# Row softmax in 17 groups: the scaling multiply moved from VectorE to GpSimd, except in the last three groups

## The chip, the cores and the metric

The kernel runs on one core of a Trainium2 chip. The metric is the device time of one execution in microseconds (us). Each figure is the median of three runs. For the kernel before it is 161.42 us, with the three runs between 161.40 and 161.58 us. The profile is of one further execution, which took 161.41 us; the profiled span inside it is 159.6 us, so some 1.8 us of the measured time lie outside the span. All times in profile lines count from the start of that span.

## What is computed

The reference is a softmax over the last axis of a float32 array of 16 x 1024 x 512, that is, over 16384 rows of 512 numbers:

```python
def reference(x):                       # x: (16, 1024, 512) float32
    x_max = np.max(x, axis=-1, keepdims=True)
    exp_x = np.exp(x - x_max)
    return (exp_x / np.sum(exp_x, axis=-1, keepdims=True)).astype(np.float32)
```

The array is 33.55 MB. It is read once and the result, of the same size, is written once.

## The kernel before

The 16384 rows are spread over 128 partitions, so each partition handles 128 rows of 512 numbers. In what follows "a row" means one such row on all 128 partitions at once: a tile of 128 x 512 numbers, 256 KB. The rows come in ten chunks. The second number of each pair is the place in the SBUF buffer, which holds 96 rows; the last two chunks reuse places of earlier ones.

```python
CHUNKS = [
    (3, 0), (5, 3), (8, 8), (16, 16), (16, 32), (16, 48), (16, 64), (16, 80), (16, 0), (16, 16),
]
EARLY = 8                          # chunks 0 to 7 are loaded at once
AFTER_STORE = {2: [8], 3: [9]}     # chunk 8 is loaded after the store of chunk 2, chunk 9 after that of chunk 3
GROUP = 8
FINISH_BEFORE = (1, 2, 3)
STORE_ROWS = {3: 8, 4: 8, 5: 8}
```

Work goes by groups of at most eight rows: one group of 3, one of 5, and fifteen of 8, numbered 0 to 16. Chunks of 16 rows are two groups. In chunks 3, 4 and 5 each group is stored by itself; in chunks 6 to 9 the store waits for both groups.

Each group passes through three steps. VectorE takes the negated maximum of each row. ScalarE computes the exponentials in place, one instruction per row, and with it the row sums. VectorE then takes the reciprocals of the sums and multiplies each row by its own. The load instructions are issued from SyncE's queue, the store instructions from ScalarE's:

```python
    def rowmax(g):
        ...
        nc.vector.reduce_max(out=shift[g], in_=place[k][:, a:b, :], axis=AX, negate=True)

    def exps(g):
        ...
        for r in range(a, b):
            nc.scalar.activation(
                out=place[k][:, r, :], in_=place[k][:, r, :], func=EXP,
                bias=shift[g][:, r - a : r - a + 1], scale=1.0,
                accum_out=sums[g][:, r - a : r - a + 1],
            )

    def scale(g):
        ...
        nc.vector.reciprocal(out=recip, in_=sums[g])
        for r in range(a, b):
            nc.vector.tensor_scalar_mul(
                out=place[k][:, r, :], in0=place[k][:, r, :],
                scalar1=recip[:, r - a : r - a + 1],
            )
        if since is not None:
            nc.scalar.dma_start(out=dst[k][:, since:b, :], in_=place[k][:, since:b, :])
        ...
```

Each engine works through its instructions in the order of the program. The order is that of this loop: scale of a group comes one group late, after the exponentials of the next; only ahead of chunks 1, 2 and 3 is the group in hand finished first.

```python
        for g, (k, a, _, _) in enumerate(groups):
            if waiting is not None and a == 0 and k in FINISH_BEFORE:
                scale(waiting)
                waiting = None
            rowmax(g)
            exps(g)
            if waiting is not None:
                scale(waiting)
            waiting = g
        scale(waiting)
```

A store instruction stands in ScalarE's order and waits there until the rows are scaled, so the exponentials behind it wait too.

Of the kernel before, what the change touches and what calls it, by code (L numbers as in the profile page):

```python
# [1 line left out]

# [4 lines left out]

F32 = mybir.dt.float32
EXP = mybir.ActivationFunctionType.Exp
AX = mybir.AxisListType.X  # L10


CHUNKS = [
    (3, 0), (5, 3), (8, 8), (16, 16), (16, 32), (16, 48), (16, 64), (16, 80), (16, 0), (16, 16),
]
SBUF_ROWS = 96

EARLY = 8
AFTER_STORE = {2: [8], 3: [9]}

GROUP = 8

FINISH_BEFORE = (1, 2, 3)

STORE_ROWS = {3: 8, 4: 8, 5: 8}

ON_ACT = ()

AT_HEAD = {mybir.EngineType.SP: 3}

def loads_at_the_head(nc):

    main, body = nc.main_func.blocks[0], nc.main_func.blocks[1]
    for engine, count in AT_HEAD.items():
        loads = [
            i
            for i in body.instructions
            if i.engine == engine and type(i).__name__ == "InstDMACopy"  # L40
        ][:count]
        barrier = next(
            n
            for n, i in enumerate(main.instructions)
            if i.engine == engine and type(i).__name__ == "InstDrain"
        )
        for load in loads:
            body.instructions.remove(load)
        main.instructions[barrier:barrier] = loads


def one_barrier_on_exit(nc):


    end = nc.main_func.blocks[2].instructions

    def of(engine, kind):
        return [i for i in end if i.engine == engine and type(i).__name__ == kind]

    for engine in (  # L60
        mybir.EngineType.Activation,
        mybir.EngineType.PE,
        mybir.EngineType.DVE,
        mybir.EngineType.SP,
    ):
        arrivals = [i for i in of(engine, "InstDrain") if i.has_update()]
        leaves = of(engine, "InstEventSemaphore")
        assert len(arrivals) == len(leaves) == 2
        end.remove(leaves[0])
        end.remove(arrivals[1])  # L70
    gather, release, gather_2, release_2 = of(mybir.EngineType.Pool, "InstEventSemaphore")
    end.remove(release)
    end.remove(gather_2)

@with_exitstack
def kernel(
    ctx: ExitStack,
    tc: tile.TileContext,
    x: bass.AP,
    out: bass.AP,  # L80
):
    nc = tc.nc
    nc.at_finalize(loads_at_the_head)
    nc.at_finalize(one_barrier_on_exit)
    P = nc.NUM_PARTITIONS

    x_flat = x.flatten_outer_dims()
    out_flat = out.flatten_outer_dims()
    n, d = x_flat.shape
    assert n == P * sum(R for R, _ in CHUNKS)  # L90


    src, dst, at = [], [], 0
    for R, _ in CHUNKS:
        for flat, views in ((x_flat, src), (out_flat, dst)):
            part = flat[at : at + P * R, :]
            views.append(part.rearrange("(p r) d -> p r d", r=R))
        at += P * R

    data = ctx.enter_context(tc.tile_pool(name="data", bufs=1))  # L100
    stats = ctx.enter_context(tc.tile_pool(name="stats", bufs=4))
    held = data.tile([P, SBUF_ROWS, d], F32, name="held")
    place = [held[:, s : s + R, :] for R, s in CHUNKS]


    groups = []
    for k, (R, _) in enumerate(CHUNKS):
        m = -(-R // GROUP)
        cuts = [R * i // m for i in range(m + 1)]
        since = 0  # L110
        for a, b in zip(cuts, cuts[1:]):
            ends = b == R or b - since >= STORE_ROWS.get(k, R)
            groups.append((k, a, b, since if ends else None))
            since = b if ends else since
    shift = [None] * len(groups)
    sums = [None] * len(groups)

    def load(k):
        queue = nc.scalar if k in ON_ACT else nc.sync
        queue.dma_start(out=place[k], in_=src[k])  # L120

    def rowmax(g):
        k, a, b, _ = groups[g]
        shift[g] = stats.tile([P, b - a], F32, name="shift", tag="shift")
        nc.vector.reduce_max(  # L125
            out=shift[g], in_=place[k][:, a:b, :], axis=AX, negate=True
        )

    def exps(g):
        k, a, b, _ = groups[g]  # L130
        sums[g] = stats.tile([P, b - a], F32, name="sums", tag="sums")
        for r in range(a, b):
            nc.scalar.activation(  # L133
                out=place[k][:, r, :],
                in_=place[k][:, r, :],
                func=EXP,
                bias=shift[g][:, r - a : r - a + 1],
                scale=1.0,
                accum_out=sums[g][:, r - a : r - a + 1],
            )  # L140

    def scale(g):
        k, a, b, since = groups[g]
        recip = stats.tile([P, b - a], F32, name="recip", tag="recip")
        nc.vector.reciprocal(out=recip, in_=sums[g])  # L145
        for r in range(a, b):
            nc.vector.tensor_scalar_mul(  # L147
                out=place[k][:, r, :],
                in0=place[k][:, r, :],
                scalar1=recip[:, r - a : r - a + 1],  # L150
            )
        if since is not None:
            nc.scalar.dma_start(
                out=dst[k][:, since:b, :], in_=place[k][:, since:b, :]
            )
        if b == CHUNKS[k][0]:
            for later in AFTER_STORE.get(k, ()):
                load(later)

    with tc.manual_schedule():  # L160
        for k in range(EARLY):
            load(k)
# [13 lines that stand above are left out]
# [1 line left out]
_INS = ['x']  # L177
_OUTS = [((16, 1024, 512), 'float32')]


# [23 lines left out]
```

## Time and profile before

| what | value |
|---|---|
| device time, median of 3 | 161.42 us (161.40 to 161.58) |
| profiled span | 159.6 us |
| VectorE busy | 123.9 us (78% of the span) |
| ScalarE busy | 93.3 us (58%) |
| GpSimd busy | 0.2 us (four small memsets) |
| bytes moved by DMA | 67.13 MB, 421 GB/s over the span |
| last store issued at | 144.93 us |

Busy times are sums of instruction durations per engine. The DMA line of the profile gives, for 40 equal slices of the span, how busy the 16 DMA engines were on average, in tenths; the line below it gives the rate of bytes moved. A groups line names the source line, the engine, the operation, the tiles written and read, the number of instructions, and after the bar the total busy time and the mean duration of one. The chain of work that ended last is followed back from the last instruction, at each step to what released it.

### The profile page before, as it was taken

The page shows a single profiled execution, that of the slowest core. Times are in us where ns is not written, and L with a number is a line of the kernel's source. Part 1 is how long each engine was busy: PE and PEld are TensorE (multiplying, and loading weights), DVE is VectorE, ACT ScalarE, POOL GpSimd, SP SyncE. Part 2 cuts the span into 40 slices and gives each one's busy share as a digit, 9 for nine tenths or more (in the row PEclk, how much of TensorE's full clock was granted, in tenths as well). Part 3 has the DMA queues.
Part 4 walks back from the last instruction along what each step waited for, and adds up shares of the span by engine and source line. Part 5 has one row for each costly group of instructions (what it writes and reads, how often), then busy time and mean ns, then how long its engine had stood idle before and what let it go on. Part 6 is the DMA issues. An engine that isn't in the chain of part 4 may idle for free.

```text
span 159.6 us, 511 instructions
## 1 busy us (share of the span) xinstructions
DVE 123.9 (78%) x162; ACT 93.3 (58%) x257; POOL 0.2 (0%) x4
## 2 busy tenths in 40 slices
DVE  0482880799699999999999999999999999853000
ACT  0717119207994959595958687776868595940000
POOL 0000000000000000000000000000000000000000
DMA  7999999899999999999899999999999999999993
GB/s 267 443 456 432 399 414 466 375 404 467 411 446 411 485 419 396 439 411 493 378 448 439 411 497 411 405 444 402 435 444 485 411 402 468 435 402 419 485 411 164
DMA packets 3315, 67.13 MB, mean 421 GB/s; under 512 B 368, under 2 KB 368, under 8 KB 624
## 3 DMA queue, kind: packets, MB, share of 16 engines
q1 hardware_dynamic: 1440, 33.56, 49.4%
q10 hardware_dynamic: 1872, 33.56, 49.0%
q14 instruction: 3, 0.02, 0.0%
HBM read 33.55 MB, written 33.55 MB: 421 GB/s over the span
## 4 chain that ended last, share of the span: by engine, by line
DVE 71%; ACT 14%; issue 3%; DMA 3%; DVEq 0%; ACTq 0%
DVE shift L125 39%; DVE held L147 30%; ACT held L133 14%; DMA held<-in_x_dram 3%; DVE recip L145 2%; DVEq L199 0%; ACTq L133 0%
## 5 line engine op out<-in xcount | busy, mean ns | idle before, releaser
L133 ACT ACTIVATE held<-held,shift 128x512 f32<-128x512 f32 x128 | 90.5, 708 | 43.4 <-DVE shift L125 33.3
L125 DVE TENSOR_REDUCE shift<-held 128x8 f32<-128x4096 f32 (+2 forms) x17 | 70.7, 4164 | 4.6 <-DMA held<-in_x_dram 4.6
L147 DVE TENSOR_SCALAR held<-held,recip 128x512 f32<-128x512 f32 x128 | 52.2, 482 | 0.6
L133 ACT ACTIVATION_READ_ACCUMULATOR held<-held,shift 128x1 f32 x128 | 23.9, 187 | 0.0
L145 DVE RECIPROCAL recip<-sums 128x8 f32<-128x8 f32 (+2 forms) x17 | 3.3, 195 | 15.8 <-ACT held L133 15.8
L133 ACT ACT_TABLE_LOAD x1 | 1.3, 1283 | 4.7 <-DMA held<-in_x_dram 4.7
L188 POOL MEMSET const-bfloat16-1.0<- 128x1 bf16 x1 | 0.1, 103 | 0.0
L188 POOL MEMSET const-uint8-127<- 128x1 uint8 x1 | 0.1, 102 | 0.0
L188 POOL MEMSET const-float32-1.0<- 128x1 f32 x1 | 0.1, 100 | 0.0
L188 POOL MEMSET const-float32-0.0<- 128x1 f32 x1 | 0.1, 99 | 0.2 <-issue 0.2
## 6 DMA issues: line engine op xcount, KB each, us to landing
held<-in_x_dram SPq DMA_DIRECT2D x7, 4096.0 KB, 41.8
out_dram<-held ACTq DMA_DIRECT2D x4, 4096.0 KB, 20.9
out_dram<-held ACTq DMA_DIRECT2D x7, 2048.0 KB, 35.3
held<-in_x_dram SPq DMA_DIRECT2D x1, 2048.0 KB, 11.7
held<-in_x_dram SPq DMA_DIRECT2D x1, 1280.0 KB, 7.2
out_dram<-held ACTq DMA_DIRECT2D x1, 1280.0 KB, 19.9
held<-in_x_dram SPq DMA_DIRECT2D x1, 768.0 KB, 4.6
out_dram<-held ACTq DMA_DIRECT2D x1, 768.0 KB, 15.6
```

The costliest lines, as they stand in the source:

```text
L125: nc.vector.reduce_max(out=shift[g], in_=place[k][:, a:b, :], axis=AX, negate=True)
L133: nc.scalar.activation(out=place[k][:, r, :], in_=place[k][:, r, :], func=EXP, bias=shift[g][:, r - a : r - a + 1], scale=1.0, accum_out=s ...
L145: nc.vector.reciprocal(out=recip, in_=sums[g])
L147: nc.vector.tensor_scalar_mul(out=place[k][:, r, :], in0=place[k][:, r, :], scalar1=recip[:, r - a : r - a + 1],)
L188: nc = _bacc.Bacc("TRN2", target_bir_lowering=False, num_devices=1)
```

## The change

GpSimd, which has nothing to do in the kernel before, takes over the multiplication of the rows by their reciprocal sums in groups 0 to 13, 104 of the 128 rows. In the last three groups (24 rows) VectorE keeps it. The reciprocals stay on VectorE in all groups. The purpose is to take work from VectorE, the busiest compute engine, and give it to an idle one.

```diff
+ON_VECTOR = 3
 ...
         nc.vector.reciprocal(out=recip, in_=sums[g])
+        engine = nc.gpsimd if g < len(groups) - ON_VECTOR else nc.vector
         for r in range(a, b):
-            nc.vector.tensor_scalar_mul(
+            engine.tensor_scalar_mul(
                 out=place[k][:, r, :],
                 in0=place[k][:, r, :],
                 scalar1=recip[:, r - a : r - a + 1],
```

Nothing else changes: loads, stores, buffers and the order on ScalarE are the same. The stores of groups 0 to 13 now wait for GpSimd.

## The prediction

> **What bounds the kernel now.** I start with the page: busy times, the DMA slices, the queues.
>
> ```profile
> DVE 123.9 (78%) x162; ACT 93.3 (58%) x257; POOL 0.2 (0%) x4
> ...
> DMA  7999999899999999999899999999999999999993
> GB/s 267 443 456 432 399 414 466 375 404 467 411 446 411 485 419 396 439 411 493 378 448 439 411 497 411 405 444 402 435 444 485 411 402 468 435 402 419 485 411 164
> ...
> HBM read 33.55 MB, written 33.55 MB: 421 GB/s over the span
> ```
>
> VectorE is the busiest compute engine at 78%, but the DMA engines are at 9 tenths in nearly every slice; only the first and the last show a gap. The table of busy time by stretch of 20 us puts numbers on it (columns: length, busy time of VectorE, ScalarE and GpSimd with instruction counts, clock, DMA share, GB/s):
>
> ```profile
> 4.00:24.00 20.00, 12.53 (x13) 7.91 (x20) 0.00 (x0) 1.00 1.02 428
> 24.00:44.00 20.00, 13.44 (x15) 12.11 (x36) 0.00 (x0) 1.00 1.00 423
> 44.00:64.00 20.00, 19.93 (x27) 15.71 (x45) 0.00 (x0) 1.00 1.01 433
> 124.00:144.00 20.00, 17.42 (x27) 13.40 (x38) 0.00 (x0) 1.00 0.98 424
> 144.00:160.00 16.00, 0.90 (x3) 0.00 (x0) 0.00 (x0) 1.00 0.84 363
> ```
>
> The DMA share is 0.98 to 1.02 whether VectorE is busy for 12.5 us of 20 or for 19.9. So **the bytes are the bound**, and VectorE, which is full in the middle, runs just fast enough to feed them. How closely it feeds them is seen in the DMA view from 145 us on, after the last store has been issued (144.93 us):
>
> ```profile
> DMA packets 195, 5.34 MB, mean 356 GB/s; under 512 B 32, under 2 KB 32, under 8 KB 32
> ...
> out_dram<-held ACTq DMA_DIRECT2D x1, 4096.0 KB, 14.0
> ```
>
> 5.34 MB were still to move, of which the last store itself is 4.19 MB (4096 KB). So 1.15 MB of earlier work was queued: at 0.432 MB/us, the mean rate of the stretches from 44 to 124 us, that is **2.7 us of reserve**. If the last store came over 2.7 us later, DMA would run dry; if it came earlier, DMA would just have a longer queue.
>
> The chain that ended last (start, us, what) and the groups by shape show the pace of compute:
>
> ```profile
> 53.87 4.33 DVE shift L125
> 58.20 0.12 DVE recip L145
> 58.32 0.02 issue
> 58.34 3.26 DVE held L147 x8
> 61.60 4.33 DVE shift L125
> ```
>
> ```profile
> L133 ACT ACTIVATE held<-held,shift 128x512 f32<-128x512 f32 x128 | 90.5, 708 | 43.4 <-DVE shift L125 33.3 <-issue 10.2
> L125 DVE TENSOR_REDUCE shift<-held 128x8 f32<-128x4096 f32 x15 | 66.1, 4414 | 0.0
> L147 DVE TENSOR_SCALAR held<-held,recip 128x512 f32<-128x512 f32 x128 | 52.2, 482 | 0.6
> ```
>
> One group of eight rows takes VectorE 61.60 - 53.87 = 7.73 us: 4.33 maximum, 0.12 of reciprocal not overlapped, 3.26 multiplies. DMA needs 8 x 2 x 0.262 MB / 0.432 = 9.7 us for the same rows in and out. The chain names VectorE because it is followed through instructions; it doesn't show that the bytes alone would take as long.
>
> **What the Trainium skill says.** (1) GPSIMD Engine Reference, section 3.1, "Elementwise — side-by-side cycle accounting": a tight loop runs at about 1.8 cycles an element, 769 ns measured for 512 elements; a simple body can reach 1.03 cycles, and an operation with two tensor inputs needs 2.6. This trace has no GpSimd arithmetic to compare with. (2) SBUF — State Buffer, "Who interferes with whom": a `tensor_reduce` never contends with GpSimd for the shared port, a `tensor_scalar` in a two-port mode does. The multiply here seems to be in it: eight take 3.26 us, 0.41 us each, where the maximum, one element at a time, needs 4414 / 8 = 552 ns a row. The reductions should be undisturbed; only the 16 multiplies of groups 14 and 15 can meet GpSimd. (3) DMA: Bandwidth & Descriptors, "Specifications": a fabric ceiling of 435 GB/s. The trace agrees: 423 to 441 GB/s in every stretch of 20 us. (4) Perfetto Trace Analysis, "GPSIMD Engine Instruction": time GpSimd by start-to-start spacing, which I shall do.
>
> **The change, part by part.** Call T the start-to-start time of one GpSimd multiply.
>
> Removed from VectorE: 104 multiplies at 3.26 / 8 = 0.41 us, 42 us. Its pace falls to 4.33 + 0.2 = 4.5 us a group. ScalarE needs 5.76 us for eight rows (the chain has it once near the end), GpSimd 8T. Reads and writes stay at 67.1 MB, 155.4 us at 0.432 MB/us, so a faster pace gains nothing once DMA is full.
>
> Added: GpSimd's 104T. From two terms of the page, an estimate of T: 769 ns plus about 60 ns for dispatch (what 4497 ns for a two-input operation on 2048 elements leaves over 2048 x 2.6 / 1.2 GHz) is 0.83 us. At 1.03 cycles it would be 0.5, at 2.6 it would be 1.17.
>
> Moved onto a path: the first groups are finished one by one. Group 0 reaches the multiply at 8.86 us as now. From there exponentials take 3.64 us (5 rows) and 5.76 (8 rows), the reciprocal with its waits 0.24, and the three first multiplies 3T, 5T and 8T. While T is under 0.93 the next maximum hides part of them. Group 3's multiply starts at 8.86 + 3T + 3.88 + 5T + 6.0 + 8T + 6.0 = 24.7 + 16T (for T of 0.83, with the maxima, 38.5 us; now 42.88). From there GpSimd runs back to back, as long as 8T is over ScalarE's pace: group 12, the last whose store holds up ScalarE alone, ends 80T later, at **24.7 + 96T**. Behind it stand the exponentials of groups 14, 15 and 16, a store issue, a reciprocal and eight multiplies on VectorE: 3 x 5.76 + 0.36 + 0.22 + 3.26 = 21.1 us. The last store goes out at 45.8 + 96T.
>
> Now it goes out at 144.9, with 2.7 us of reserve. So 45.8 + 96T = 147.6 gives **T = 1.06 us as the break-even**. At 0.83 the last store goes out at about 126 us (130 if the last load, which now ends near 109 us, is waited for), DMA has a queue of some 15 us more, and the end is set by bytes alone.
>
> Sum at the central T: the 155.4 us of bytes stay; the start (0.72 DMA share in the first 4 us) and the last store's receipt stay. What can be won are the slightly thin stretches, 423 and 424 GB/s against 432: 20 x (1 - 423.5/432) = 0.4 us each, 0.8 together, of which I count half. 161.4 - 0.4 = **161.0 us**.
>
> **Rivals.** (a) *GpSimd becomes the bound*, T over 1.06. For: GpSimd is a software engine, the per-row waits are many, and I have no measured T. Against: the multiply has one tensor input, and the page's 2.6 cycles are for two. The time rises by 9.6 us for each 0.1 us of T: past the break-even, the end is the last store + 4.19/0.432 = 9.7, + 2.3 us of latency and receipt (now 159.6 - 144.93 - 5.34/0.432), + 1.8 us outside the span. T = 1.1: last store 151.4, time 165.2. T = 1.17: 158.1, time 172. (b) *VectorE was the bound and its relief shows*: the chain and the 19.9 us of 20 speak for it. If so, one would gain up to 7.73 - 6.64 = 1.1 us a group over ten groups, 11 us, to 150. Against: the DMA share of 1.0 and 155.4 us of bytes; I give it almost nothing. (c) *A collision at the shared port* in groups 14 and 15: 16 multiplies each blocked by one of T would be 13 us, but at T = 0.83 there is a queue of at least 15 us to hide it. It would matter only near the break-even.
>
> **Range and chances.** The DMA-bound outcome (T under 1.0) I hold to be three in four, at 160 to 161.6 us. T between 1.0 and 1.1 gives 161 to 165, T above up to 175. The low end is 159.6: all of the thin stretches and a little of the tail; the high end 168, T of 1.13. Under 158.2 (2% faster) would need more than 440 GB/s throughout: 0.04. Over 164.6 needs T over 1.09: 0.22.
>
> **What would show it.** GpSimd starts 0.8 us apart (right below 1.0, wrong above); its busy time near 86 us; group 3's multiply begins at about 38 us; VectorE busy 124 - 104 x 0.48 = 74 us; maxima still at 4414 ns; the last store issued between 125 and 135 us, and more than 10 MB left at that point; DMA at 9 in all slices but the first and the last. A DMA digit that falls before the end, with ScalarE waiting for GpSimd, would mean rival (a). The prediction would also fail if bytes moved faster or slower under another mix of reads and writes.

## The result, and the profile after

The changed kernel takes **214.8 us** (213.94 to 214.86) against 161.42 us. The ratio is 1.329, with a 95% interval from 1.326 to 1.333. It is a third slower; the prediction said 161.0 us in a range from 159.6 to 168.0.

Busy times, DMA slices and bytes of the page after:

```profile
DVE 85.3 (40%) x58; ACT 92.9 (44%) x257; POOL 161.9 (76%) x108
...
DMA  8999999999999999999976245000990029669496
GB/s 319 432 431 427 394 456 415 457 400 445 437 400 437 462 412 449 399 434 449 308 308 295 98 179 217 0 0 0 394 394 0 0 98 394 295 297 394 197 394 295
...
HBM read 33.55 MB, written 33.55 MB: 315 GB/s over the span
```

The same bytes are moved. For the first half of the span the DMA engines are as full as before. From the 21st slice on, about 106 us, they run dry again and again. GpSimd, idle before, is busy for 161.9 us. The stretches of 20 us show the turn (columns as in the prediction: length, busy time of VectorE, ScalarE and GpSimd, clock, DMA share, GB/s):

```profile
84.00:104.00 20.00, 6.96 (x3) 8.99 (x25) 20.00 (x14) 1.00 1.06 430
104.00:124.00 20.00, 9.01 (x4) 8.25 (x24) 20.00 (x14) 1.00 0.51 216
124.00:144.00 20.00, 9.01 (x4) 11.38 (x32) 20.00 (x14) 1.00 0.25 105
```

While loads are still queued, slow stores go unnoticed here. The last load has landed at 107 us; after that the DMA engines have only stores to move, which wait for GpSimd, and its column reads 20.00 of 20. The groups by shape give the cost of one multiply on each engine:

```profile
L150 POOL TENSOR_SCALAR held<-held,recip 128x512 f32<-128x512 f32 x104 | 161.7, 1621 | 25.8 <-DVE recip L147 25.8
L135 ACT ACTIVATE held<-held,shift 128x512 f32<-128x512 f32 x128 | 90.4, 708 | 100.2 <-POOL held L150 94.1 <-DVE shift L127 6.1
L127 DVE TENSOR_REDUCE shift<-held 128x8 f32<-128x4096 f32 x15 | 65.7, 4386 | 0.0
...
L150 DVE TENSOR_SCALAR held<-held,recip 128x512 f32<-128x512 f32 x24 | 13.0, 614 | 0.1
```

ScalarE now waits 94.1 us for GpSimd: its store instructions wait for scaled rows, and the exponentials stand behind them. In the chain that ended last (start, us, what) GpSimd has taken VectorE's place:

```profile
58.65 23.58 POOL held L150 x16
82.23 1.06 issue
83.28 23.58 POOL held L150 x16
...
132.58 23.62 POOL held L150 x16
156.19 0.99 issue
...
174.28 0.34 ACTq L156
...
180.79 5.37 DVE held L150 x7
...
187.30 4.34 DVE shift L127
...
191.72 5.76 ACT held L135 x16
```

From 58.65 to 83.28 GpSimd does 16 rows: 24.63 / 16 = **1.54 us a row**, where the estimate was 0.83. The 23.58 are only the part during which instructions are recorded as running. The pace is the same where the DMA engines are full and where they mostly stand still: from 132.58 us on, 16 rows take 23.62 + 0.99 = 24.61 us. So the transfers don't slow it. Nor do VectorE's maxima: row by row in the same trace, GpSimd's multiplies start 1.54 us apart beside a maximum and while VectorE rests.

### The profile page after: what moved, and what is told of

Same layout as the page of the kernel before. It is cut to its first block, busy times and chain, and to the rows that moved or that the text cites. A ratio compares the mean times of both kernels' runs of the same rounds, so it can differ in the third digit from the quotient of the medians.

```text
span 212.9 us, 540 instructions
## 1 busy us (share of the span) xinstructions
DVE 85.3 (40%) x58; ACT 92.9 (44%) x257; POOL 161.9 (76%) x108
## 3 DMA queue, kind: packets, MB, share of 16 engines
q1 hardware_dynamic: 1440, 33.56, 37.7%
q10 hardware_dynamic: 1872, 33.56, 36.9%
## 4 chain that ended last, share of the span: by engine, by line
POOL 63%; ACT 11%; issue 10%; DVE 7%; DMA 2%; POOLq 1%; ACTq 1%; DVEq 0%
POOL held L150 63%; ACT held L135 11%; DVE held L150 4%; DVE shift L127 2%; DMA held<-in_x_dram 2%; POOLq L202 1%; ACTq L156 0%; DVE recip L147 0%; DVEq L202 0%; ACTq L135 0%; POOLq L150 0%; DVEq L147 0%; DVEq L150 0%
## 5 line engine op out<-in xcount | busy, mean ns | idle before, releaser
L150 POOL TENSOR_SCALAR held<-held,recip 128x512 f32<-128x512 f32 x104 | 161.7, 1621 | 25.8 <-DVE recip L147 25.8
L135 ACT ACTIVATE held<-held,shift 128x512 f32<-128x512 f32 x128 | 90.4, 708 | 100.2 <-POOL held L150 94.1
L150 DVE TENSOR_SCALAR held<-held,recip 128x512 f32<-128x512 f32 x24 | 13.0, 614 | 0.1
```

The lines of the kernel that those rows point to most:

```text
L135: nc.scalar.activation(out=place[k][:, r, :], in_=place[k][:, r, :], func=EXP, bias=shift[g][:, r - a : r - a + 1], scale=1.0, accum_out=s ...
L150: engine.tensor_scalar_mul(out=place[k][:, r, :], in0=place[k][:, r, :], scalar1=recip[:, r - a : r - a + 1],)
```

## The experiments

In what follows T is GpSimd's time a row from start to start. The edits are against the changed kernel. "Last store" is when the last store is issued. Times are medians of 4 to 12 executions, except those marked as one run; ratios are to the kernel before, timed again alongside (161.48 to 161.51 us).

### What makes a GpSimd multiply take 1.54 us

**One instruction for two rows.** Both rows are multiplied by the reciprocal of the first, so nearly half of the 104 rows are scaled by another row's value.

```diff
-        for r in range(a, b):
+        wide = 2 if engine is nc.gpsimd else 1
+        for r in range(a, b, wide):
+            e = min(r + wide, b)
             engine.tensor_scalar_mul(
-                out=place[k][:, r, :], in0=place[k][:, r, :],
+                out=place[k][:, r:e, :].rearrange("p r d -> p (r d)"),
+                in0=place[k][:, r:e, :].rearrange("p r d -> p (r d)"),
                 scalar1=recip[:, r - a : r - a + 1],
```

> Each GpSimd multiply covers two rows (128x1024) with the reciprocal of the first; a lone row is left over in the groups of 3 and 5. Question: is the 1.54 us from start to start paid per element or per instruction? Theory A, per element (a loop on the engine, 512 elements in 1.54 us): a 128x1024 multiply takes 2.9 to 3.1 us, the time stays at 210 to 215 us. Rival B, per instruction (dispatch, semaphore wait, fetch of the scalar; the loop itself 0.77 us as my estimate had it): 128x1024 takes 1.54 + 0.77 = 2.3 us, GpSimd's pace falls to 9.2 us a group and the time to 24.7 + 96 x 1.155 + 27 + 12 + 1.8 = about 176 us.

The time is 202.25 us (one run). GpSimd's timeline (start, us, engine, line, operation, tiles, count):

```profile
49.25 124.55 POOL L152 TENSOR_SCALAR held<-held,recip 128x1024 f32<-128x1024 f32 x44 [6.55 <-DVE recip L147]
```

124.55 / 44 = 2.83 us for 1024 elements, 1.54 for 512. The difference is 1.29 us for 512 elements, 2.52 ns an element; 0.25 us is left as the cost of an instruction. Theory A holds in the main: 84% of the time is paid per element. Both figures fell below A's windows (2.9 us, and 210 us for the time), so the cost of an instruction isn't nothing.

**A constant in place of the reciprocal.** The scaling by the sums is left out in groups 0 to 13.

```diff
-                scalar1=recip[:, r - a : r - a + 1],
+                scalar1=0.5 if engine is nc.gpsimd else recip[:, r - a : r - a + 1],
```

> GpSimd multiplies by the constant 0.5 and no longer reads the reciprocals. Question: does the per-partition scalar operand make the multiply slow? If it does, the multiply falls towards the 0.83 us that I had estimated and the time to 161 to 165 us. If the loop over the elements is the cost (theory A), it stays within 10% of 1.54 us and the time between 200 and 215 us.

```profile
34.65 128.62 POOL L150 TENSOR_SCALAR held<-held 128x512 f32<-128x512 f32 x88 [1.37 <-ACT held L135]
```

128.62 / 88 = 1.46 us a row. Reading the scalar from each partition costs 0.08 us, no more. The time of 190.92 us (one run) lies below the window of 200 to 215, mostly for another reason: without a wait for the reciprocals GpSimd begins its 88 rows at 34.65 us and not at 50.95.

**A copy, no arithmetic.** Each row of groups 0 to 13 is copied onto itself; its scaling is left out.

```diff
         for r in range(a, b):
+            if engine is nc.gpsimd:
+                engine.tensor_copy(out=place[k][:, r, :], in_=place[k][:, r, :])
+                continue
             engine.tensor_scalar_mul(
             ...
```

> GpSimd only copies each row onto itself; the scaling of groups 0 to 13 is left out. Question: what does GpSimd need for 512 elements with one input and no arithmetic? Theory A, the multiply by a scalar is itself a slow routine (2.5 ns an element, where the two-tensor multiply takes 1.7): the copy is far quicker, 0.5 to 0.8 us a row, and the time is at the level of the bytes, 161 to 162 us. Rival, reading or writing a row is what takes 1.5 us for one-input forms: 1.4 us or more a row, and 190 us or more.

```profile
42.68 11.18 POOL L151 COPY held<-held 128x512 f32<-128x512 f32 x16 [0.79 <-ACT held L135]
```

11.18 / 16 = 0.70 us a row, and 161.43 us (one run). So reading and writing 512 elements doesn't take 1.5 us. The slowness belongs to GpSimd's multiply by a scalar, not to every operation with one input.

**The multiply as one operation on two tensors per group.** The reciprocals are repeated along each row by the access pattern. The result is the full softmax.

```diff
-        for r in range(a, b):
+        if engine is nc.gpsimd:
+            engine.tensor_mul(
+                out=place[k][:, a:b, :],
+                in0=place[k][:, a:b, :],
+                in1=recip[:, :, None].to_broadcast([P, b - a, d]),
+            )
+        for r in range(a, b) if engine is nc.vector else ():
             engine.tensor_scalar_mul(
             ...
```

> One GpSimd multiply of two tensors per group, the reciprocals repeated along each row: no per-row instruction and no scalar operand, but two inputs. If the skill's 2.6 cycles an element hold, a row takes 512 x 2.6 / 1.2 GHz = 1.11 us, a group 8.9 us, and the time is 24.7 + 96 x 1.11 + 27 + 12 + 1.8 = 172 us: slower than before and far faster than the change. If GpSimd's loop costs the same whatever the form (1.54 us a row or more), the time is 214 us or more.

It takes **161.49 us**, a ratio of 1.000 to the kernel before (0.999 to 1.001). GpSimd's timeline has three sizes:

```profile
8.79 2.75 POOL L150 TENSOR_TENSOR held<-held,recip 128x1536 f32<-128x1536 f32 x1 [8.36 <-DVE recip L147]
15.98 4.46 POOL L150 TENSOR_TENSOR held<-held,recip 128x2560 f32<-128x2560 f32 x1 [4.44 <-DVE recip L147]
26.97 7.02 POOL L150 TENSOR_TENSOR held<-held,recip 128x4096 f32<-128x4096 f32 x1 [6.53 <-DVE recip L147]
```

They lie on a line: (7.02 - 2.75) / 2560 = 1.67 ns an element, and 0.19 us an instruction. These are recorded durations; where eleven follow each other they start 6.98 us apart. A row costs 0.87 us (6.98 / 8), little more than half of the scalar form's 1.54, though it reads two tensors. I had expected 172 us, from 2.6 cycles an element; at the 1.2 GHz of the Trainium skill, GPSIMD Engine Reference, section 1, 1.67 ns are 2.0 cycles, and section 3.1's 2.6 doesn't hold for this repeated operand. The scalar form's 2.52 ns are 3.0 cycles.

**The same with one instruction per row.**

```diff
         for r in range(a, b):
+            if engine is nc.gpsimd:
+                engine.tensor_mul(
+                    out=place[k][:, r, :],
+                    in0=place[k][:, r, :],
+                    in1=recip[:, r - a : r - a + 1].to_broadcast([P, d]),
+                )
+                continue
             engine.tensor_scalar_mul(
             ...
```

> The two-tensor multiply on GpSimd, but one instruction per row as in the change: 104 of them. The three sizes of the run with one multiply per group lie on 0.19 us plus 1.67 ns an element. Theory, form and count are separate costs: a row takes 0.19 + 512 x 0.00167 = 1.04 us from start to start, just at the break-even (1.06 by the prediction, 1.01 with the tail of 25.5 us that the slower runs show), so the last store goes out at about 150 us, 2 to 3 us beyond the reserve, and the time is 162 to 165 us. Rival, it is the number of instructions that made the change slow: 1.3 us or more a row and 185 us or more.

```profile
42.51 87.80 POOL L151 TENSOR_TENSOR held<-held,recip 128x512 f32<-128x512 f32 x88 [6.53 <-DVE recip L147]
```

T is 87.80 / 88 = 1.00 us, and the time 161.61 us, a ratio of 1.000 (0.999 to 1.001), just under the expected 162 to 165. With as many instructions as the change has, in the same places, the loss is gone. So the number of instructions isn't the cause, the form is. The last store goes out at 147.18 us, just inside the 147.6 that the prediction computed as the last harmless moment; I had expected it at 150.

### Where the break-even lies

**Part of each group on GpSimd.** In groups 0 to 13 GpSimd takes the first four rows of a group with the slow scalar form, in a second run the first six, and VectorE the others. The edit for four (for six, `4` is `6`):

```diff
         for r in range(a, b):
-            engine.tensor_scalar_mul(
+            on = engine if r - a < 4 else nc.vector
+            on.tensor_scalar_mul(
```

> In groups 0 to 13 GpSimd takes only the first four rows, VectorE the other four. GpSimd then needs 4 x 1.54 = 6.2 us a group, under the 8.5 us of the break-even (8 x 1.06). Theory: it was GpSimd's rate alone, so the time is back at the level of the bytes, 161 to 164 us. Rival, the shared port: in the change VectorE's eight multiplies beside GpSimd took 6.51 us and not 3.26; if each of the four here waits for a whole GpSimd multiply, VectorE's group is 4.4 + 0.2 + 4 x (1.54 + 0.41) = 12.4 us, and the time 195 us or more. At 0.81 us each, as in group 14, it is 7.9 us and the time 161 to 165.

With four rows: 161.79 us, a ratio of 1.0015 (1.0007 to 1.0024). VectorE's timeline in such a group:

```profile
65.15 2.46 DVE L151 TENSOR_SCALAR held<-held,recip 128x512 f32<-128x512 f32 x4
```

Four multiplies take 2.46 us where four at 0.41 would take 1.6. There is a collision, but it doesn't cost a whole GpSimd multiply each time, and VectorE's group stays under 7 us (the next four start at 72.07). GpSimd is slowed as well: its group takes 76.11 us for 44 rows / 11 = 6.92 us and not the 6.2 expected, still under 8.5. So the rate theory holds.

> In groups 0 to 13 GpSimd takes six rows of each eight, VectorE two. Theory, the chain of waits with its break-even at 8.5 us of GpSimd work a group: 6 x 1.54 = 9.24 us a group is over it, group 12 ends at 24.7 + 14 x 1.54 + 10 x 9.24 = 139 us, the last store goes out some 25 us later, at 164, and the time is 164 + 11.8 + 1.8 = 177 us (174 to 180). Rival, a balance of rates: DMA needs 9.7 us for eight rows in and out, so anything quicker than that a group is hidden and the time stays at 161 to 163 us.

With six rows: **181.29 us**, a ratio of 1.122 (1.121 to 1.124). GpSimd's timeline:

```profile
48.24 104.13 POOL L151 TENSOR_SCALAR held<-held,recip 128x512 f32<-128x512 f32 x66 [6.55 <-DVE recip L147]
```

104.13 / 11 = 9.47 us a group (1.58 us a row on average, since some collide with VectorE's multiplies). That is quicker than the 9.7 us that DMA needs for eight rows in and out, and still costs 20 us. The rival, a balance of rates, falls: loads and stores don't come in step. The loads run ahead and have landed by 110 us, with 20.6 MB of stores still to move. From there DMA gets only the 2.10 MB that GpSimd's pace allows each 9.47 us, and is half empty:

```profile
124.00:144.00 20.00, 12.20 (x8) 12.19 (x35) 20.00 (x13) 1.00 0.55 236
```

The chain theory holds, though it sat 4 us low: the store after group 12 went out at 142.75 (139 expected), the last 24.9 us later, and the time lies just above the expected 174 to 180.

### The start and the tail

**No serial start.**

```diff
-FINISH_BEFORE = (1, 2, 3)
+FINISH_BEFORE = ()
```

> The change with the list of chunks ahead of which the group in hand is finished first left empty, so the first groups overlap. In the change GpSimd stood idle for 17.6 us between its first four groups. Theory, GpSimd's own work is the bound and that serial start comes on top: GpSimd begins at about 10 us, ends its 104 rows at 172 to 174 us (187.9 in the change), and the time falls by 14 us, to 200 us (197 to 203). Rival, the serial start is hidden beside the loads: 212 us or more.

```profile
10.60 4.64 POOL L150 TENSOR_SCALAR held<-held,recip 128x512 f32<-128x512 f32 x3 [10.18 <-DVE recip L147]
17.10 7.72 POOL L150 TENSOR_SCALAR held<-held,recip 128x512 f32<-128x512 f32 x5 [1.85 <-DVE recip L147]
27.82 149.04 POOL L150 TENSOR_SCALAR held<-held,recip 128x512 f32<-128x512 f32 x96 [3.00 <-DVE recip L147]
```

The time is 202.98 us, at the upper end of the expected 197 to 203. GpSimd's idle time between its first groups falls from 17.6 to 4.9 us, its start is 1.9 us later, and it ends at 176.9 instead of 187.9 us (172 to 174 expected). The 11.8 us gained show that the serial start is on the path once GpSimd is the bound; the larger part of the loss remains.

**Group 13 on VectorE too.**

```diff
-ON_VECTOR = 3
+ON_VECTOR = 4
```

> Group 13 goes back to VectorE as well, so GpSimd is idle when VectorE multiplies group 14. Theory, the shared port: group 14's eight multiplies take 3.26 us again where they took 6.51 beside GpSimd, the last store goes out 3.2 us sooner (201.1 to 197.9) and the time falls from 214.8 to 211.5 us. Rival, no collision (the 6.51 us come from something else, or the tail waits for the store of group 12's chunk alone): no change of more than 1 us.

VectorE's multiplies of groups 13 and 14 in this run:

```profile
161.69 5.68 DVE L150 TENSOR_SCALAR held<-held,recip 128x512 f32<-128x512 f32 x8
...
182.22 3.26 DVE L150 TENSOR_SCALAR held<-held,recip 128x512 f32<-128x512 f32 x8
```

and of groups 14 and 15 in the changed kernel:

```profile
180.79 6.51 DVE L150 TENSOR_SCALAR held<-held,recip 128x512 f32<-128x512 f32 x8
...
191.77 3.26 DVE L150 TENSOR_SCALAR held<-held,recip 128x512 f32<-128x512 f32 x8
```

Eight VectorE multiplies take 3.26 us when GpSimd rests, and 5.7 to 6.5 us beside its multiplies. Group 14's collision went away as expected, but group 13's now strikes GpSimd in group 12, whose store goes out 1.4 us later (175.69 for 174.28). So the last store comes 1.8 us sooner and the time is 212.92 us, 1.9 us less; I had expected 3.3. The collision costs both sides.

### Can the bytes be moved faster?

With the two-tensor multiply, stores of 16 rows in all large chunks:

```diff
-STORE_ROWS = {3: 8, 4: 8, 5: 8}
+STORE_ROWS = {}
```

> One two-tensor multiply per group on GpSimd, which left 10 us of unused lead, and all stores of 16 rows instead of 8 in chunks 3 to 5, so that the packets of the stores are 32 KB like those of the loads. Theory, the bytes are the bound at a rate that packets of 16 or 32 KB share: 161.4 us, within 0.3% of before. Rival, the smaller packets cost rate: 159.5 to 160.5 us, faster than both kernels.

The packets of the store queue fall from 1872 to 1440, as many as the loads have. The time is 161.91 us, a ratio of 1.0027 (1.0017 to 1.0036): a trifle slower, so larger stores don't raise the rate. No run here beats the kernel before.

## Why the prediction was wrong

| GpSimd's work | T or us a group | store after group 12 | last store | time |
|---|---|---|---|---|
| none (before) | - | 115.76 | 144.93 | 161.42 |
| two-tensor, one per group | T 0.87 | 110.33 | 134.07 | 161.49 |
| two-tensor, one per row | T 1.00 | 122.36 | 147.18 | 161.61 |
| scalar form, six of eight rows | 9.47 a group | 142.75 | 167.63 | 181.29 |
| scalar form, all rows (the change) | T 1.54 | 174.28 | 201.10 | 214.8 |

- **The step that failed is the size of T**: "From two terms of the page, an estimate of T ... is 0.83 us". It was taken from a figure for a tight loop whose operation the cited page doesn't name, and no trace tied it to this multiply. Measured: 1.54 us, of which 0.25 a fixed part and 1.29 for the elements. The argument against rival (a), that one tensor input must be cheaper than two, was wrong in its sign here: the scalar form needs 2.52 ns an element, the two-tensor form 1.67. And with no T in the trace, a range that ended at T = 1.13 was too sure.
- **The chain built on T was right in its mechanism.** Group 3's multiply: 24.7 + 16 x 1.54 = 49.3, measured 50.95. Group 12's end: 24.7 + 96 x 1.54 = 172.5, its store measured at 174.28. From last store to the end: 212.9 - 201.1 = 11.8, predicted 12.0. With the true T the formulas give 45.8 + 147.8 + 12.0 + 1.8 = 207.4 us, against 214.8. Of the 7.4 us between, 1.8 had gathered by group 12 and 5.7 came behind it.
- **The tail (the time from group 12's store to the last one) was 5.7 us too short**: 21.1 predicted, 201.10 - 174.28 = 26.8 measured. It had two gaps. It took ScalarE's three groups as back to back, while the chain shows group 16's maximum (187.30, 4.34 us) waiting behind group 14's multiplies on VectorE. And rival (c), the collision with VectorE's multiplies, which I had left out of the sum, added 3.25 us to those of group 14; group 15's took 3.26 as ever. So it was far smaller than the 13 us of rival (c). With one two-tensor multiply per group, where hardly anything collides, the tail is 134.07 - 110.33 = 23.7 us: the first gap is about 2.6 us, the collision the rest.
- **The break-even was nearly right**: 1.06 predicted. The formula 45.8 + 96T puts the last store about 5 us too early in the harmless runs too (129.3 for 134.07 at T of 0.87, 141.8 for 147.18 at 1.00), so the reserve is all but used up at T of 1.00, where nothing is lost yet. Past it each late microsecond counts in full: time minus last store is 13.7 us both with six rows and in the change.
- **What bounds the kernel before was read right, and rival (b) is dead.** With the two-tensor multiply the last store goes out 10.9 us sooner, and the time doesn't move. In the stretch from that store on, 10.06 MB were left, where the kernel before had 5.34 (the prediction's sign asked for more than 10):

```profile
DMA packets 355, 10.06 MB, mean 388 GB/s; under 512 B 48, under 2 KB 48, under 8 KB 48
```

One reading was loose: the prediction has the trace agree with a ceiling of 435 GB/s, but the stretch from 104 to 124 us of the kernel before moved 441. The measurement decides.

- **The 0.4 us gain from thin stretches** doesn't exist: 161.43 us (the copy, one run) and 161.49 us with a faster feed.
- **VectorE's busy time** was to be 74 us and is 85.3. I took 482 ns a multiply; neighbours overlap, so each fills only 0.41 us. 124 - 104 x 0.41 is 81; the collision adds 3.25, which leaves under 1 us.
- **The maxima were undisturbed**, as the Trainium skill says in SBUF — State Buffer, "Who interferes with whom": 4386 ns each on average in the change, 4414 in the kernel before. That the collision of the multiplies is one at the shared port fits this, but no run here shows the port itself.

What stays open is why GpSimd's multiply by a scalar needs three cycles an element; no run looked inside it.

## What to carry to other kernels

Before moving work to an idle engine, measure that exact form of instruction there: the same multiply cost GpSimd 1.54 us a row as a multiply by a scalar, 1.00 as a two-tensor multiply, and 0.87 batched over eight rows. Work out how late the last store may go out (bytes left behind it times the rate) and turn that into the longest duration that the new engine may need: here 1.0 us a row, and the runs in the table fell on the side that it says. In this kernel, where the transfers are the bound, relieving the busy compute engine brought nothing, and slowing the feed cost nothing until the queue was empty, then all of it.

## What the runs showed of the hardware that I had not expected

- On GpSimd, two tensor inputs, one of them repeated by the access pattern, are faster than one input and a scalar: 1.67 against 2.52 ns an element. A constant instead of the per-partition scalar saves only 0.08 us of 1.54, and a copy of a row takes 0.70 us.
- Beside GpSimd's multiplies, eight VectorE multiplies stretch from 3.26 to between 5.7 and 6.5 us, less than if each waited for a whole GpSimd multiply (8 x 1.54 = 12.3 us more), and GpSimd is delayed too, by 1.4 us over a group.
